# By-token products for gates, merge and MLP of a hybrid decoder block, with seven block products in place of eight in three of the eight k pairs of the MLP's first product

## The chip, the core and the metric

The kernel runs on one core of a Trainium2 chip, in fp32. TensorE (PE) multiplies: a 128x128 stationary operand is loaded (PEld), and up to 512 columns of a moving operand stream through it into a PSUM bank of 128x512 fp32, of which there are eight. VectorE (DVE) and ScalarE (ACT) work element by element, GpSimd (POOL) does a little of that and issues some DMAs, SyncE (SP) issues the loads of the weights. The metric is device time in microseconds (us) of one execution.

## The reference, cut to what matters

For 256 tokens of 2048 features:

```
h = rms_norm(x) ; proj = h @ w_in                      # 2048 x 18576
gate_att, gate_ssm, q, k, v, q_idx, k_idx, w_idx, z, xbc, dt = split(proj)
att = top-k sparse attention(q, k, v, q_idx, k_idx, w_idx)     # 16 heads
y   = gated, normed state-space mixer(z, conv(xbc), dt)        # 4096 wide
merged = sigmoid(gate_att) * (att @ w_att) + sigmoid(gate_ssm) * (y @ w_ssm)
x = x + merged @ w_out
x = x + square(relu(rms_norm(x) @ w_up)) @ w_down      # w_up 2048 x 8192
```

## The kernel before

Each fp32 operand is split into a rounded part `hi` (fp32r) and a rest `lo`; a product is hi\*hi + hi\*lo + lo\*hi. `split` (L106, L107) makes the two parts of a weight chunk of 128x1024: a copy on ACT and a difference on DVE. `load` (L115) fetches the chunk through SP's queue into one of four `raw` buffers; `hi` and `lo` have three buffers each.

There are two forms of matrix product. `gemm_t` gives the result by feature (128 features on the partitions): for each k tile of 128 and each 128 features it takes the weights as stationary operand, `hi` against 512 moving columns (the 256 tokens' hi and lo side by side, L122) and `lo` against 256 columns (L123). Such a couple of matmuls, 512 and 256 columns, I call a pair of instructions. Its evacuation, `halves` (L175, L176), adds the two halves of the bank. `gemm_a` gives the result by token (128 tokens on the partitions): the activations are stationary and the weights move, three matmuls of 512 columns for each k tile, 128 tokens and 512 features (L148). For 128 tokens x 512 features x 128 k that is 1536 columns; `gemm_t` streams 768 columns for 256 tokens x 128 features x 128 k, so both forms stream the same number of columns for the same work, in 3 instructions by token and 4 by feature.

By feature run: the index queries, the two gate projections (`C_GA`, `C_GS`), B, C and x of the mixer, `w_att`, `w_ssm`, `w_out` and `w_up`. By token run q, k, v, z and `w_down`. At the start x is loaded by token into `xt` and turned on PE by 32 transposes (L285); g1\*x is the moving operand of the first two groups, while `h_first` (L340 to L343) makes the normed `hl` that all later products use; a small product of 144 columns (L408, L410) follows. In the MLP `u` holds all 64 tiles of 128 hidden features by 256 tokens; `w_down` runs after that in two halves of its output columns over 64 k tiles, each bank started by four transposes of the residual (L950, 32 in all).

Work beside the products (scores, heads, the mixer, the convolution) is written as generators; `pump` runs a step of them after each chunk, by a credit of the stage. A scheduler then sets the order of each engine's instructions from its own timeline, except on DVE and ACT in the first group, which is written in order by hand. Two of the PSUM banks serve such side work (`aux_bank`), six the products (`main_bank`).

## Time and profile before

| | |
|---|---|
| median of 3 runs | 2000.99 us (2000.95 to 2001.97) |
| profiled execution, its own time | 2002.37 us |
| its span | 2000.6 us |
| PE busy | 1993.1 us (100%), 10693 instructions |
| DVE busy | 1376.6 us (69%) |
| ACT busy | 1055.0 us (53%) |
| POOL busy | 54.3 us (3%) |
| HBM traffic | 187 GB/s over the span |

The page gives busy time and share of each engine, a strip of 40 slices, the DMA queues, the chain of work that ended last, and the costliest groups of instructions. A PE instruction's own duration overlaps with the next one's, so the cost of a matmul in a row of matmuls is read from a stretch divided by its count, not from the mean of one. An fp32 matmul that is no transpose stands as two instructions in the profile.

### The profile page before, as it was taken

Reading aid. Unit: us, or ns where it says so; the run is one execution under the profiler, and the core shown is the slowest. Engines: PE = TensorE matmul, PEld = TensorE weight load, DVE = VectorE, ACT = ScalarE, POOL = GpSimd, SP = SyncE. Lnnn points to the kernel's source line nnn. Section 1 sums busy time; section 2 is a strip of 40 time slices with the busy share of each in tenths; the row PEclk is TensorE's granted clock in tenths of the full one; section 3 lists DMA queues with packets and bytes.
Section 4 is the critical chain, followed back from the end, with each engine's and each line's share of the span. In section 5 each row is a group of like instructions: output and inputs, shape, how many; then the busy total and the mean of one; then the engine's idle time right before and its main releaser. Section 6 shows DMA issues by size and latency. Waiting matters only on the chain.

```text
span 2000.6 us, 28778 instructions
## 1 busy us (share of the span) xinstructions
PE 1993.1 (100%) x10693; PEld 1702.4 (85%) x10693; DVE 1376.6 (69%) x2444; ACT 1055.0 (53%) x1730; POOL 54.3 (3%) x125
## 2 busy tenths in 40 slices
PE   9999999999999999999999999999999999999999
PEld 8878888888888888888888888888888888888887
DVE  8877766568888888888667677665555555555554
ACT  6555655444555554555656665555544445455444
POOL 2002000000000000000000000000000000000000
PEclk9999999999999999999999999999999999999999
DMA  7647555566555665555555555655555555556553
GB/s 261 201 144 220 174 160 162 170 220 190 182 183 175 187 192 175 188 183 169 190 183 189 188 188 199 201 193 189 187 191 189 189 189 190 189 191 210 194 199 133
DMA packets 172850, 375.35 MB, mean 188 GB/s; under 512 B 16787, under 2 KB 17637, under 8 KB 172709
## 3 DMA queue, kind: packets, MB, share of 16 engines
q1 hardware_dynamic: 168004, 357.97, 55.4%
q0 software_dynamic: 4704, 15.54, 2.8%
q8 instruction: 84, 1.38, 0.3%
q14 instruction: 58, 0.47, 0.1%
HBM read 368.42 MB, written 5.05 MB: 187 GB/s over the span
## 4 chain that ended last, share of the span: by engine, by line
PE 99%; DMA 0%; DVE 0%; SPq 0%; issue 0%; ACT 0%; DVEq 0%; ACTq 0%
PE mb L122 40%; PE mb L148 33%; PE mb L123 20%; PE ab L804 1%; PE ab L492 0%; PE ab L748 0%; PE ab L823 0%; PE ab L600 0%; PE ab L796 0%; PE ab L768 0%; PE ab L625 0%; DMA xt<-in_x_dram 0%; PE mb L408 0%; PE ab L621 0%; PE ab L757 0%; PE ab L599 0%
## 5 line engine op out<-in xcount | busy, mean ns | idle before, releaser
L107 DVE TENSOR_TENSOR lo<-raw,hi 128x1024 fp32r<-128x1024 f32 x664 | 811.3, 1224 | 555.8 <-ACT hi L106 552.1
L106 ACT CAST hi<-raw 128x1024 fp32r<-128x1024 f32 x664 | 697.8, 1052 | 748.1 <-PE mb L122 402.0
L122 PE MATMUL mb<-h_hl,hi 128*128 128x512 f32 x1280 | 439.9, 397 | 0.0
L122 PE MATMUL mb<-x_hl,hi 128*128 128x512 f32 x1024 | 343.4, 394 | 0.0
L123 PE MATMUL mb<-h_hl,lo 128*128 128x256 f32 x1280 | 342.0, 286 | 0.0
L148 PE MATMUL mb<-hi,uhl 128*128 128x512 f32 x1024 | 316.9, 390 | 0.0
L148 PE MATMUL mb<-hi,h_hl 128*128 128x512 f32 x896 | 280.5, 392 | 0.0
L122 PEld LDWEIGHTS mb<-h_hl,hi 128*128 128x128 f32 x1280 | 236.2, 188 | 50.5 <-issue 1.9
L123 PE MATMUL mb<-x_hl,lo 128*128 128x256 f32 x1024 | 261.6, 279 | 0.0
L123 PEld LDWEIGHTS mb<-h_hl,lo 128*128 128x128 f32 x1280 | 236.2, 189 | 8.3 <-issue 1.9
L148 PEld LDWEIGHTS mb<-hi,uhl 128*128 128x128 f32 x1024 | 192.2, 188 | 39.7
L122 PEld LDWEIGHTS mb<-x_hl,hi 128*128 128x128 f32 x1024 | 186.3, 188 | 37.8
L148 PE MATMUL mb<-lo,uhl 128*128 128x512 f32 x512 | 199.3, 389 | 0.0
L148 PEld LDWEIGHTS mb<-hi,h_hl 128*128 128x128 f32 x896 | 167.4, 188 | 36.6 <-issue 2.3
L123 PEld LDWEIGHTS mb<-x_hl,lo 128*128 128x128 f32 x1024 | 187.7, 188 | 7.2
L122 PE MATMUL mb<-yhl,hi 128*128 128x512 f32 x512 | 180.3, 398 | 0.6 <-DVE yhl L877 0.4
L148 PE MATMUL mb<-lo,h_hl 128*128 128x512 f32 x448 | 176.2, 393 | 0.0
L123 PE MATMUL mb<-yhl,lo 128*128 128x256 f32 x512 | 142.2, 280 | 0.0
L122 PEld LDWEIGHTS mb<-yhl,hi 128*128 128x128 f32 x512 | 95.8, 188 | 24.8 <-DVE yhl L877 2.1
L148 PEld LDWEIGHTS mb<-lo,uhl 128*128 128x128 f32 x512 | 96.1, 188 | 19.8
L148 PEld LDWEIGHTS mb<-lo,h_hl 128*128 128x128 f32 x448 | 84.1, 188 | 18.3 <-issue 1.3
L123 PEld LDWEIGHTS mb<-yhl,lo 128*128 128x128 f32 x512 | 96.5, 189 | 0.5
(264 smaller groups left out, 2032.0 us busy)
## 6 DMA issues: line engine op xcount, KB each, us to landing
raw<-in_w_in_dram SPq DMA_DIRECT2D x288, 512.0 KB, 3.5
raw<-in_w_down_dram SPq DMA_DIRECT2D x64, 1024.0 KB, 5.2
raw<-in_w_up_dram SPq DMA_DIRECT2D x60, 1024.0 KB, 5.2
raw<-in_w_ssm_branch_dram SPq DMA_DIRECT2D x64, 512.0 KB, 3.9
raw<-in_w_att_branch_dram SPq DMA_DIRECT2D x32, 512.0 KB, 3.8
raw<-in_w_out_dram SPq DMA_DIRECT2D x32, 512.0 KB, 4.0
abc<-acum_d POOLq DMA_DIRECT2D x16, 512.0 KB, 5.0
raw<-in_w_up_dram SPq DMA_DIRECT2D x8, 512.0 KB, 4.5
```

The costliest lines, as they stand in the source:

```text
L106: a.copy(hi, raw)
L107: v.tensor_tensor(lo, raw, hi.bitcast(F32), op=OP.subtract)
L122: pe.matmul(banks[j], hi[:, js], mv, start=kk == 0, stop=False)
L123: pe.matmul(banks[j][:, :S], lo[:, js], mv[:, :S], start=False, stop=kk == nk - 1)
L148: pe.matmul(banks[t][c], st[:, x_ + t * P:x_ + (t + 1) * P], w_[:, c * 512:(c + 1) * 512], start=kk == 0 and i == 0 and not started, stop= ...
L804: pe.matmul(yd[:, i * 64:(i + 1) * 64], M[:, i], xk[c][:, i * 64:(i + 1) * 64], start=True, stop=True)
```

## The change

- The gate projections (`C_GA`; `C_GS` in the same way, in `gates`), `w_att`, `w_ssm`, `w_out` and `w_up` are computed by token. `gemm_a` with chunks of 128x1024 takes the place of `gemm_t`; the evacuations become one operation of 512 columns per bank.
- What a later product needs by feature is turned on PE: `merged` (32 transposes, `merged_task`), the new x (32, `norm_task`), the squared hidden features (128, `u_task`).
- `w_up` is done by `mixed` in eight groups of 1024 features, over eight pairs of k tiles. For one pair, 2 token blocks x 2 feature blocks x 2 k tiles make eight block products. `UP = "NSNSNSNN"` sets the kind of a pair: N does the eight, S does seven products of sums of blocks. All of them accumulate in seven PSUM banks (`q`), so that N has to be written in S's terms: it adds into the banks 2, 5, 3 and 4 and uses the difference of the two token blocks as a third stationary operand. `combine` makes the four results of the seven banks. `left` makes the sums on the activations' side (POOL, then hi and lo), once for the kernel, `pieces_s` those on the weights' side, in every group.
- The MLP runs in two halves of its hidden features: `up(0)`, `down(0)`, `up(1)`, `down(1)`; `u` is half as large. `w_down` has the k tiles of a half, and the residual is added on DVE at its evacuation instead of by transposes on PE.
- In the MLP the PSUM banks are divided into seven for products and one for side work.
- x is handed over by feature (`x_t`), with vectors, convolution taps and the table of the attention's bias laid out; the transposes of x at the start, the small ones of the vectors and the bias product fall away. In the first group the sums of squares come from ACT and POOL on `x_t`, and the reciprocal root is made after the group.

```diff
+UP = "NSNSNSNN"
...
+                    a.activation(ssx, xT[:, :2], AF.Square)
+                else:
+                    sq = ap_.tile([P, 2, S], F32, name=nm("sq"), tag="bt", bufs=3)
+                    a.activation(sq, xT[:, k:k + 2], AF.Square)
+                    nc.gpsimd.tensor_tensor(ssx, ssx, sq, op=OP.add)
...
-        matt = low.tile([P, KT, S], F32, name="matt", tag="matt")
-        for g in range(4):
-            def ev(j, bank, g=g):
-                m = matt[:, 4 * g + j]
-                halves(ap_, bank, m)
-                a.activation(m, m, AF.Tanh, scale=0.5)
-            gemm_t(w_in, C_GA + g * 512, KT, h_mv, ev, RATE)
+        matt = low.tile([P, 2, D], F32, name="matt", tag="matt")
+        for g in range(2):
+            banks = [[main_bank(), main_bank()] for _ in range(2)]
+            for t, c in gemm_a(wide(w_in, C_GA + g * 1024), KT, h_mv, banks, RATE):
+                c0 = g * 1024 + c * 512
+                a.activation(matt[:, t, c0:c0 + 512], banks[t][c], AF.Tanh, scale=0.5)
...
-        for g in range(4):
-            def ev(j, bank, g=g):
-                t = ap_.tile([P, S], F32, name=nm("ao"), tag="ao", bufs=2)
-                halves(ap_, bank, t)
-                m = matt[:, 4 * g + j]
-                v.scalar_tensor_tensor(m, m, 1.0, t, op0=OP.add, op1=OP.mult)
-            gemm_t(w_att, g * 512, KT, lambda kk: att_hl[:, kk], ev, RATE)
+        for g in range(2):
+            banks = [[main_bank(), main_bank()] for _ in range(2)]
+            for t, c in gemm_a(wide(w_att, g * 1024), KT, lambda kk: att_hl[:, kk], banks, RATE):
+                c0 = g * 1024 + c * 512
+                m = matt[:, t, c0:c0 + 512]
+                v.scalar_tensor_tensor(m, m, 1.0, banks[t][c], op0=OP.add, op1=OP.mult)
...
+        def merged_task(g, ms):
+            for c in range(2):
+                transposed(lambda t: ms[t][c], 8 * g + 4 * c, to_mhl)
+                yield 2500
+
+        for g in range(2):
+            if g:
+                tg = gates(g)
+            banks = [[main_bank(), main_bank()] for _ in range(2)]
+            ms = [[None, None], [None, None]]
+            for t, c in gemm_a(wide(w_ssm, g * 1024), 32, y_mv, banks, 500):
+                c0 = g * 1024 + c * 512
+                m = ms[t][c] = mp.tile([P, 512], F32, name=nm("m"), tag="m", bufs=4)
+                v.scalar_tensor_tensor(m, tg[:, t, c * 512:(c + 1) * 512], 1.0, banks[t][c],
+                                       op0=OP.add, op1=OP.mult)
+                v.tensor_tensor(m, m, matt[:, t, c0:c0 + 512], op=OP.add)
+            queue.append(merged_task(g, ms))
...
+        LEFT_S = {1: 0, 2: 1, 3: 3, 5: 4, 7: 6, 6: 5, 4: 2}
+        LEFT_N = {2: (0, 0), 5: (1, 1), 3: (2, 1), 4: (1, 0)}
+
+        def left(kind, pool, src, hi, lo):
+
+            d = pool.tile([P, 4, P], F32, name=nm("d"), tag="d", bufs=2)
+            g = nc.gpsimd
+            if kind == "S":
+                a11, a12, a21, a22 = src[:, 0, 0], src[:, 1, 0], src[:, 0, 1], src[:, 1, 1]
+                g.tensor_tensor(d[:, 1], a21, a22, op=OP.subtract)
+                g.tensor_tensor(d[:, 2], d[:, 1], a11, op=OP.subtract)
+                g.tensor_tensor(d[:, 0], d[:, 2], a12, op=OP.add)
+                g.tensor_tensor(d[:, 3], a11, a21, op=OP.subtract)
+                parts = ((slice(0, 2), src[:, :, 0]), (2, a22), (slice(3, 7), d))
+            else:
+                g.tensor_tensor(d[:, :2], src[:, :, 0], src[:, :, 1], op=OP.subtract)
+                hi, lo = (z.rearrange("p (k n) t -> p k n t", n=3) for z in (hi, lo))
+                parts = (((slice(None), slice(0, 2)), src), ((slice(None), 2), d[:, :2]))
+            for at, x_ in parts:
+                at = (slice(None), *at) if isinstance(at, tuple) else (slice(None), at)
+                a.copy(hi[at], x_)
+                v.tensor_tensor(lo[at], x_, hi[at].bitcast(F32), op=OP.subtract)
...
+        def norm_task(g):
+            for j in range(4 * g, 4 * g + 4):
+                b = aux_bank()
+                for i in range(2):
+                    for t in range(2):
+                        c0 = (2 * j + i) * P
+                        pe.transpose(b[:, i * S + t * P:i * S + (t + 1) * P],
+                                     xn[:, t, c0:c0 + P], ident)
+                x_ = scratch[0].tile([P, 2, 2, P], F32, name=nm("xf"), tag="ev",
+                                     bufs=1 if scratch[0] is mp else 5)
+                for i in range(2):
+                    m = 2 * j + i
+                    a.mul(x_[:, i], b[:, i * S:(i + 1) * S].rearrange("p (t n) -> p t n", t=2),
+                          vec[:, G2 + m:G2 + m + 1])
+                z = XA[g][:, xa_at[j]:xa_at[j] + (7 if UP[j] == "S" else 6)]
+                left(UP[j], scratch[0], x_, z[:, :, :P], z[:, :, P:])
+                xa_done.add(j)
+                yield 2500
...
+        psum_stack.close()
+        psum[:] = [enter(tc.tile_pool(name="psum2", bufs=1, space=PSUM)), 7]
...
+            r0, r1 = (load(w, kk + i, 1, c0, 1024)[:, 0] for i in range(2))
+            h1 = fp.tile([P, 512], F32R, name=nm("h1"), tag="h1", bufs=1)
+            l1 = fp.tile([P, 512], F32R, name=nm("l1"), tag="l1", bufs=1)
+            a.copy(h1, r0[:, :512])
+            v.tensor_tensor(l1, r0[:, :512], h1.bitcast(F32), op=OP.subtract)
+            h2, l2 = (z[:, 0] for z in split(r1, [P, 1, 1024]))
+            t13 = fp.tile([P, 2, 512], F32, name=nm("t13"), tag="t13", bufs=1)
+            v.tensor_tensor(t13[:, 0], r0[:, :512], r0[:, 512:], op=OP.add)
+            v.tensor_tensor(t13[:, 1], r0[:, 512:], r1[:, 512:], op=OP.add)
+            h3, l3 = split(t13, [P, 2, 512])
+            t24 = fp.tile([P, 2, 512], F32, name=nm("t24"), tag="t24", bufs=1)
+            v.tensor_tensor(t24[:, 0], t13[:, 0], r1[:, 512:], op=OP.add)
+            v.tensor_tensor(t24[:, 1], t24[:, 0], r1[:, :512], op=OP.add)
+            h4 = fp.tile([P, 2, 512], F32R, name=nm("h4"), tag="h4", bufs=1)
+            l4 = fp.tile([P, 2, 512], F32R, name=nm("l4"), tag="l4", bufs=1)
+            a.copy(h4, t24)
+            v.tensor_tensor(l4, t24, h4.bitcast(F32), op=OP.subtract)
+            return {1: (h1, l1), 2: (h2[:, :512], l2[:, :512]), 3: (h2[:, 512:], l2[:, 512:]),
+                    5: (h3[:, 0], l3[:, 0]), 7: (h3[:, 1], l3[:, 1]),
...
+        def mixed(kinds, w, k0, c0, operands, rate):
+
+            q = {i: main_bank() for i in (1, 6, 7, 2, 5, 3, 4)}
+            left_of = {i: sum(1 if kind == "S" else 2 * (i in LEFT_N) for kind in kinds)
+                       for i in q}
+            total = dict(left_of)
+
+            def product(i, hi, lo, whi, wlo):
+                for n, (st, mv) in enumerate(((hi, whi), (hi, wlo), (lo, whi))):
+                    pe.matmul(q[i], st, mv, start=left_of[i] == total[i] and n == 0,
+                              stop=left_of[i] == 1 and n == 2)
+                left_of[i] -= 1
+
+            for j, kind in enumerate(kinds):
+                hi, lo = operands(j)
+                kk = k0 + 2 * j
+                if kind == "S":
+                    ws = pieces_s(w, kk, c0)
+                    for i, s_ in LEFT_S.items():
+                        product(i, hi[:, s_], lo[:, s_], *ws[i])
+                else:
+                    ws = pieces_n(w, kk, c0)
+                    last = j == len(kinds) - 1
+                    todo = [(i, k) for k in range(2) for i in LEFT_N]
+                    if last:
+                        todo.sort(key=lambda x_: list(LEFT_N).index(x_[0]))
+                    for i, k in todo:
+                        s_, c = LEFT_N[i]
+                        s_ += 3 * k
+                        cs = slice(c * 512, c * 512 + 512)
+                        product(i, hi[:, s_], lo[:, s_], ws[k][0][:, cs], ws[k][1][:, cs])
+                pump(rate)
+            return q
...
+            q1 = block()
+            a.copy(q1, q[1])
+            u2 = plus(q[6], q1)
+            u3 = plus(q[7], u2)
+            v.tensor_tensor(out_[0][0], q[2], with_(q1, 0, 0), op=OP.add)
+            t5 = plus(q[5], u2, OP.subtract)
+            if before is None:
...
+            v.tensor_tensor(out_[0][1], q[3], with_(t5, 0, 1), op=OP.add)
+            v.tensor_tensor(out_[1][0], q[4], with_(u3, 1, 0), op=OP.add)
...
+        def u_task(g, cs):
+
+            for c in range(2):
+                for t in range(2):
+                    a.activation(cs[t][c], cs[t][c], AF.Relu, scale=rstd2[:, t:t + 1])
+                for j2 in range(2):
+                    b = aux_bank()
+                    for j in range(2):
+                        for t in range(2):
+                            f0 = (2 * j2 + j) * P
+                            pe.transpose(b[:, j * S + t * P:j * S + (t + 1) * P],
+                                         cs[t][c][:, f0:f0 + P], ident)
+                    m = 8 * g + 4 * c + 2 * j2
+                    a.activation(u[:, m:m + 2], b.rearrange("p (m s) -> p m s", m=2), AF.Square)
+                    yield 5000
+
+        def up(h):
+            for g in range(4):
+                q = mixed(UP, w_up, 0, h * MH + g * 1024, x_operands, 5000)
+                cs = [[fp.tile([P, 512], F32, name=nm("c"), tag="c", bufs=4) for _ in range(2)]
+                      for _ in range(2)]
+                combine(q, cs)
+                queue.append(u_task(g, cs))
...
+        def down(h):
...
+                for t, c in gemm_a(d_pieces, MH // P, u_st, banks, 2500,
+                                   tail=2 if h and c2 else 0):
+                    c0 = c2 * 1024 + c * 512
+                    x_ = xn[:, t, c0:c0 + 512]
+                    if h == 0:
+                        v.tensor_tensor(x_, banks[t][c], x_, op=OP.add)
+                        continue
+                    o = fp.tile([P, 512], F32, name=nm("o"), tag="c", bufs=4)
+                    v.tensor_tensor(o, banks[t][c], x_, op=OP.add)
+                    nc.sync.dma_start(out2[t * P:(t + 1) * P, c0:c0 + 512], o)
+
+        for h in range(2):
+            up(h)
+            down(h)
```

Of its 10,425 matmul instructions as built the program keeps 9,201. 2560 of the 3456 pairs of `gemm_t` are gone; `gemm_a` has 5184 matmuls instead of 2880, and `mixed` (L973) has 1464.

On DVE, in `w_up` before, between two groups of 512 features: `lo` of the weight chunks, and the evacuations of the banks (`up`).

```order
L176 TENSOR_TENSOR up_2666_14215<-mb_2640_14033,half_2667_14216 128x256
L933 SCALAR_TENSOR_TENSOR up_2664_14209<-up_2664_14209,rb2_12135 128x256
L933 SCALAR_TENSOR_TENSOR up_2666_14215<-up_2666_14215,rb2_12135 128x256
L107 TENSOR_TENSOR lo_2681_14276<-raw4_2679_14273,hi_2680_14275 128x1024
L176 TENSOR_TENSOR up_2668_14221<-mb_2641_14034,half_2669_14222 128x256
L933 SCALAR_TENSOR_TENSOR up_2668_14221<-up_2668_14221,rb2_12135 128x256
L107 TENSOR_TENSOR lo_2683_14296<-raw4_2679_14273,hi_2682_14295 128x1024
L107 TENSOR_TENSOR lo_2686_14318<-raw4_2684_14315,hi_2685_14317 128x1024
```

On DVE, in `w_up` now, in a group's third and fourth pair of k tiles (N, then S): `raw_2351` and `raw_2354` are the N pair's chunks, `raw_2358` and `raw_2359` the S pair's; `t13` and `t24` are sums of weight blocks, `l1` and `l4` the rests of the blocks that have no `lo` buffer.

```order
L950 TENSOR_TENSOR t13_2364_12211<-raw_2358_12199 128x512
L951 TENSOR_TENSOR t13_2364_12211<-raw_2358_12199,raw_2359_12201 128x512
L111 TENSOR_TENSOR lo_2353_12160<-raw_2351_12157,hi_2352_12159 128x1024
L954 TENSOR_TENSOR t24_2367_12218<-t13_2364_12211,raw_2359_12201 128x512
L947 TENSOR_TENSOR l1_2361_12204<-raw_2358_12199,h1_2360_12203 128x512
L111 TENSOR_TENSOR lo_2356_12166<-raw_2354_12163,hi_2355_12165 128x1024
L1077 TENSOR_TENSOR uhl_2585_13171<-u_11623,uhl_2585_13171 128x256
L955 TENSOR_TENSOR t24_2367_12218<-t24_2367_12218,raw_2359_12201 128x512
L1077 TENSOR_TENSOR uhl_2591_13206<-u_11623,uhl_2591_13206 128x256
L111 TENSOR_TENSOR lo_2363_12208<-raw_2359_12201,hi_2362_12207 128x1024
L111 TENSOR_TENSOR lo_2366_12215<-t13_2364_12211,hi_2365_12214 128x1024
L959 TENSOR_TENSOR l4_2369_12222<-t24_2367_12218,h4_2368_12221 128x1024
```

The two `lo` of the N pair have the sums for the S pair between them, and ahead of PE's use `uhl` tiles of the coming `w_down`. Where two chunks gave two rows before, an S pair now gives eight.

On PE, in `w_up` before, at a group's k tile: four banks (`mb_2670` to `mb_2673`) in turn.

```order
L122 MATMUL mb_2670_14227<-x_hl_12133,hi_2682_14295 128x512
L122 MATMUL mb_2671_14228<-x_hl_12133,hi_2682_14295 128x512
L122 MATMUL mb_2672_14229<-x_hl_12133,hi_2682_14295 128x512
L122 MATMUL mb_2673_14230<-x_hl_12133,hi_2682_14295 128x512
L123 MATMUL mb_2670_14227<-x_hl_12133,lo_2683_14296 128x256
L123 MATMUL mb_2671_14228<-x_hl_12133,lo_2683_14296 128x256
L123 MATMUL mb_2672_14229<-x_hl_12133,lo_2683_14296 128x256
L123 MATMUL mb_2673_14230<-x_hl_12133,lo_2683_14296 128x256
```

On PE, in `w_up` now, at the first pair of k tiles (N) of the second group: `mb_2326` to `mb_2329` are the banks 2, 5, 3 and 4 of the group.

```order
L973 MATMUL mb_2326_12048<-hi_2334_12060,xa0_10901 128x512
L973 MATMUL mb_2327_12049<-hi_2334_12060,xa0_10901 128x512
L973 MATMUL mb_2328_12050<-hi_2334_12060,xa0_10901 128x512
L973 MATMUL mb_2326_12048<-lo_2335_12061,xa0_10901 128x512
L973 MATMUL mb_2326_12048<-hi_2334_12060,xa0_10901 128x512
L973 MATMUL mb_2327_12049<-lo_2335_12061,xa0_10901 128x512
L973 MATMUL mb_2327_12049<-hi_2334_12060,xa0_10901 128x512
L973 MATMUL mb_2328_12050<-lo_2335_12061,xa0_10901 128x512
L973 MATMUL mb_2328_12050<-hi_2334_12060,xa0_10901 128x512
L973 MATMUL mb_2329_12051<-hi_2331_12054,xa0_10901 128x512
L973 MATMUL mb_2329_12051<-lo_2332_12055,xa0_10901 128x512
L973 MATMUL mb_2329_12051<-hi_2331_12054,xa0_10901 128x512
```

Three of the group's banks are taken in turn, and the fourth, `mb_2329`, comes 18 matmuls later than the first: it is the bank that waits for a result of the group before to be read.

## Rows read from the trace of the kernel before

**Rows 1.** The page: busy time of engines; granted clock; the chain that ended last.

```profile
PE 1993.1 (100%) x10693; PEld 1702.4 (85%) x10693; DVE 1376.6 (69%) x2444; ACT 1055.0 (53%) x1730; POOL 54.3 (3%) x125
...
PEclk9999999999999999999999999999999999999999
...
PE 99%; DMA 0%; DVE 0%; SPq 0%; issue 0%; ACT 0%; DVEq 0%; ACTq 0%
```

**Rows 2.** Busy time (count) in stretches: mixer, w_up, w_down; clock, DMA share, GB/s.

```profile
408.00:955.00 547.00, 547.00 (x3004) 468.76 (x3003) 448.79 (x927) 278.37 (x408) 18.67 (x64) 1.00 0.59 185
1273.00:1630.00 357.00, 357.00 (x2049) 311.71 (x2048) 208.37 (x281) 178.36 (x264) 0.00 (x0) 1.00 0.59 190
1630.00:2000.60 370.60, 366.23 (x1651) 303.82 (x1649) 207.24 (x267) 180.28 (x267) 0.00 (x0) 1.00 0.55 187
```

**Rows 3.** The chain that ended last: start us, us, engine, tile, line, count.

```profile
921.91 0.87 PE ab L823 x8
...
1825.72 170.52 PE mb L148 x752
```

**Rows 4.** PE's groups by line and shape: count, busy us, mean ns.

```profile
L122 PE MATMUL mb<-h_hl,hi 128*128 128x512 f32 x1280 | 439.9, 397 | 0.0
L122 PE MATMUL mb<-x_hl,hi 128*128 128x512 f32 x1024 | 343.4, 394 | 0.0
...
L122 PE MATMUL mb<-yhl,hi 128*128 128x512 f32 x512 | 180.3, 398 | 0.6 <-DVE yhl L877 0.4
...
L122 PE MATMUL mb<-att_hl,hi 128*128 128x512 f32 x256 | 87.7, 398 | 0.1
L122 PE MATMUL mb<-mhl,hi 128*128 128x512 f32 x256 | 85.3, 396 | 0.0
...
L950 PE MATMUL mb<-ident,xn 128*128 128x128 f32 x32 | 5.1, 272 | 0.0
...
L285 PE MATMUL ab<-ident,xt 128*128 128x128 f32 x16 | 3.5, 355 | 0.9 <-DMA xt<-in_x_dram 0.9
...
L285 PE MATMUL mb<-ident,xt 128*128 128x128 f32 x16 | 2.5, 281 | 0.3 <-DMA xt<-in_x_dram 0.3
```

**Rows 5.** DVE's groups by line and shape: count, busy us, mean ns, idle before.

```profile
L107 DVE TENSOR_TENSOR lo<-raw,hi 128x1024 fp32r<-128x1024 f32 x664 | 811.3, 1224 | 555.8 <-ACT hi L106 552.1 <-PE ab L588 1.3 <-PE mb L122 1.1
...
L806 DVE TENSOR_TENSOR y<-ab,y 128x512 f32<-128x512 f32 x16 | 11.0, 687 | 0.1
...
L340 DVE SCALAR_TENSOR_TENSOR h<-xT,vec,rb 128x256 f32<-128x256 f32 x16 | 7.6, 479 | 0.0
...
L343 DVE TENSOR_TENSOR h_hl<-h,h_hl 128x256 fp32r<-128x256 f32 x16 | 6.4, 419 | 0.0
...
L189 DVE SCALAR_TENSOR_TENSOR rs_t<-rs_t,rs_m 128x2 f32<-128x2 f32 x27 | 4.2, 157 | 0.3
...
L403 DVE TENSOR_TENSOR hi<-raw,hi 128x288 fp32r<-128x288 f32 x8 | 3.6, 450 | 0.4 <-ACT hi L402 0.2
```

**Rows 6.** ACT's groups by line and shape: count, busy us, mean ns, idle before.

```profile
L106 ACT CAST hi<-raw 128x1024 fp32r<-128x1024 f32 x664 | 697.8, 1052 | 748.1 <-PE mb L122 402.0 <-PE mb L148 284.7 <-issue 39.9
```

**Rows 7.** DMA issues: count, KB each, median us from issue to landing.

```profile
raw<-in_w_in_dram SPq DMA_DIRECT2D x288, 512.0 KB, 3.5
...
raw<-in_w_out_dram SPq DMA_DIRECT2D x32, 512.0 KB, 4.0
...
xt<-in_x_dram SPq DMA_DIRECT2D x4, 128.0 KB, 3.3
```

**Rows 8.** The start in order of time: start us, us, what.

```profile
8.06 2.07 PE L122 MATMUL mb<-xg,hi 128*128 128x512 f32 x4
```

**Rows 9.** Line 408: duration ns min/median/max, first and last start us.

```profile
L408 PE MATMUL mb<-hi,h_hl x32: 293/340/377, 58.0 to 65.6; 128*128 128x288 f32 x32
```

**Rows 10.** DVE's groups from 10 to 25 us, where POOL is busy.

```profile
L306 DVE TENSOR_TENSOR lo<-raw,hi 128x1024 fp32r<-128x1024 f32 x5 | 9.5, 1899 | 0.0
```

**Rows 11.** The same stretch, busy time (count) of PE, PEld, DVE, ACT, POOL.

```profile
10.00:25.00 15.00, 14.68 (x93) 12.82 (x93) 13.72 (x20) 13.14 (x31) 10.39 (x8) 1.00 0.99 352
```

373 lines of the change are left out of this document (166 added, 207 removed).

## The prediction, made before the changed kernel ran

> **What bounds the kernel now.** I read the page first [rows 1]. PE is busy 1993.1 of 2000.6 us, the chain that ended last is 99% PE, and the granted clock is full, which is the 2.4 GHz level, from end to end. DVE (69%) and ACT (53%) have room. So a PE instruction taken away is time taken away, as long as DVE keeps up. Then I read the stretches [rows 2]: even in the mixer, where DVE is busy 448.8 of 547.0 us (82%), PE is busy for the whole 547.0. In `w_up` DVE is busy 58% and POOL does nothing. Third, I read what a PE instruction costs in a row of its like: the `w_up` stretch holds 2049 PE instructions in 357.00 us, that is 1024 pairs of 512 and 256 columns, 348.6 ns a pair [rows 2]; `w_down`, by token, has 752 matmuls of 512 columns in 170.52 us, 226.8 ns each [rows 3].
>
> **Part 1: by feature to by token.** A pair streams 768 columns, which is 1.5 matmuls by token, 340.1 ns. The gain is 8.5 ns a pair. The pairs that go are the counts of 512-column matmuls [rows 4]: 512 of the 1280 from `h_hl` (both gates), 256 `att_hl`, 512 `yhl`, 256 `mhl`, 1024 `x_hl`, in sum 2560. That is 2560 x 8.5 ns = **-21.8 us**.
>
> The Trainium skill ("TensorE: Matmul & The Clock Gate", section "Back-to-back issue gap") gives for an isolated warm matmul the columns divided by 2.4, plus 2.5 ns: an estimate from it is 325 ns for a pair and 323.8 for 1.5 matmuls, a gain of 1.3 ns and 3.3 us in all, and the kernel would come out at 1999.7. The stretches above are 5% longer than that in both forms and differ more among themselves. The measurement decides.
>
> **Part 2: seven products for eight.** Eight groups with three S pairs each leave out one block product of three matmuls: 72 matmuls x 226.8 ns = **-16.3 us**. An N pair has its 24 matmuls as `gemm_a` would; the detour through S's banks adds none.
>
> **Part 3: transposes.** A row of eight 128-column transposes took 0.87 us, 108 ns each [rows 3]. Added are 32 (`merged`), 32 (x) and 128 (`u`); removed are 32 of L950 and 32 of L285 (16 into `ab`, 16 into `mb`) [rows 4]. Net 128 x 108 ns = **+13.8 us**. The small transposes of vectors and taps and the bias product go too: I take **-1** (0 to -2).
>
> **Part 4: the head.** The first product started at 8.06 us [rows 8], behind x's transposes. Now x comes by feature, and a 128 KB piece of x lands 3.3 us after its issue [rows 7], so some 5.5 us is possible. That is 2.5 us, and the transposes that stood among the first products (32 x 0.108 = 3.5 us in all) go. Against it stands DVE. The reciprocal root is now made behind the first group, and only then `h_first` can run: 16 x (479 + 419) ns = 14.4 us. With it are due eight `lo` (9.8 us), eight operations on banks at about 0.42 (3.3), the small product's eight splits (3.6), and the root and its spreading (about 2.8): 34 us of DVE [rows 5], while PE has one group of about 22 us and no other work. The small product's last matmul started at 65.6 us [rows 9]; I expect 61.5: **-4** (0 to -6).
>
> **Part 5: DVE in the new `w_up`.** This is where the gain can be lost. For a group of 1024 features DVE has 10 `lo` for five N pairs and 9 for three S pairs, 19 x 1.224 us, and 22 operations of 512 columns (l1 and four sums in each S pair, seven in `combine`). The trace has no sum of two SBUF operands of that width; I price them by `y` of 128x512, 687 ns, and not by half of a `lo`, 612 [rows 5]. In sum 23.3 + 15.1 = 38.4 us. PE has 183 matmuls and 16 transposes, 41.5 + 1.7 = 43.2 us. So DVE is 89% busy, above the mixer's 82%. ACT has about as many elements to cast at 1052 ns and stays near 27 us of 43 [rows 6]; it is no rival. Inside the group it isn't even: an S pair needs 7.1 us of DVE for 4.76 of PE, an N pair 2.45 for 5.44. N stands before S so that DVE can work ahead, as far as the four `raw` and three `lo` buffers let it; `h1`, `l1`, `t13`, `t24`, `h4` and `l4` have one buffer each. I walked the built order through a group with these durations: PE waits some 0.25 us for the first S pair's `h3`, and some 0.6 us for the first `lo` of the fifth pair, together 0.9 a group. At the group's start PE enters three banks and comes to the fourth 18 matmuls (4.1 us) later, and `combine` has read that one after about 2.3 us; no stall there. The first group also has the `left` work on DVE for the S pairs (about 7 us with the root of the second norm): 45.4 of DVE against 43.2 of PE, 2.2 us late. Stalls: 2.2 + 7 x 0.9 = **+8.5** (0 to 54.5, the top being rival A's).
>
> POOL has a part here. In the stretch from 10 to 25 us POOL is busy 10.39 of 15 us [rows 11], and a `lo` took 1899 ns instead of 1224 [rows 10]: five of them lose 3.4 us, a third of POOL's busy time. POOL now makes `left`'s differences (some 3.4 us of POOL in the first group) and, in the head, the sums of squares. By the row DVE loses about 1.1 us in the first group, which is in the 2.2 above.
>
> The Trainium skill ("SBUF — State Buffer", section "Who interferes with whom") says that a DVE operation with two SBUF inputs and a GpSimd operation that reads SBUF exclude each other on a shared port pair. The row shows a third of that; by the rule the whole 3.4 us would be lost once, and the forecast would be 2.3 us higher.
>
> **Part 6: the rest.** The PSUM pools change hands ahead of the MLP, and `down(0)` and `down(1)` each begin on banks that `combine` has to free: **+1** (0 to 2). Weights are read as often as before. A 512 KB chunk lands 3.5 to 4.0 us after issue [rows 7] and `w_up` moved 190 GB/s at a DMA share of 0.59 [rows 2]; in a kernel 1% shorter that grows by 1%. `w_down`'s residual moves from PE to an operation that replaces an evacuation of equal size, and costs nothing.
>
> **Sum.** -21.8 - 16.3 + 13.8 - 1 - 4 + 8.5 + 1 = -19.8 us. The profiled execution has a span of 2000.6 and an own time of 2002.37, 1.4 above the median of the runs. I take its differences from the median: 2000.99 - 19.8 = **1981**.
>
> **Rivals.**
> *A, DVE sets the pace in `w_up`.* With one buffer for `t13`, `t24`, `h4` and `l4`, at each of the 24 S pairs PE waits for a cast (1.05) [rows 6] and a difference (1.22) [rows 5] made only after the buffer is free: 24 x 2.27 = 54.5 in place of 8.5, **2027**. It turns the change slower as soon as a pair costs more than (19.8 + 8.5) / 24 = 1.2 us. For it: 89% busy, S pairs that need 7.1 us of DVE in 4.76 of PE. Against it: N pairs between them give back 3 us each, the mixer at 82% didn't wait, and in the order the next S pair's sums stand among the N pair's `lo`.
> *B, the conversion gives nothing.* If the 8.5 ns belong to what ran beside the two stretches (`w_up` against `w_down`) and not to the form, part 1 is 0: **2003**. For it: the two rates come from different stretches. Against it: the `w_down` stretch has as much DVE work (207 us) and 187 GB/s [rows 2], and is the faster. The Trainium skill's formula of part 1 would end close to B; by that formula neither stretch would have its length.
> *C, no stall, and the head gains 6.* 1981 - 8.5 - 2 - 1 and a little from the vectors: **1968** or less.
> *That the change doesn't do what it says* is not open: as built it has 9,201 matmul instructions for 10,425 and L973's 1464 is 1536 less 72.
>
> **How the numbers follow.** Forecast (stalls of 0 to 2.5 us a group): 1968 to 1996, chance 0.66. A: 0.22, of which 0.07 within 0.2% (4 us, about what a measurement here can tell from no change) and 0.15 above. B: 0.07, same. C below 1968: 0.05. Faster 0.71, same 0.14, slower 0.15. The range runs from 1968 to 2004, leaving out C and the upper part of A, 0.2.
>
> **What would show it.** The cadence of L152 and L973 in an unbroken row should be 227 ns, and the stretches of the gates, `w_att`, `w_ssm` and `w_out` shorter by 2.4% plus their transposes at 108 ns; a cadence of 232 is B. A group of `w_up` should take about 44 us with DVE busy at 85 to 90%; PE's waits should name `lo` (L111), `h3` and `l4` (L959). If a group takes 50 us, A is right. The small product should end at about 62 us. The prediction is wrong if a sum of 512 columns costs far more than 687 ns, or if PE is slower between banks that change with every third matmul than in `w_down`.

## The result, and the profile of the changed kernel

The changed kernel takes 1988.39 us (median of 4 runs, 1988.21 to 1988.68) against 2001.48 us of the kernel before beside it (2000.95 to 2002.49): ratio 0.9936, 95% interval 0.9923 to 0.9948. That is 13.1 us faster, where 19.8 were forecast; the time lies in the range. The profiled execution has a span of 1987.0 us, 13.6 less than the 2000.6 of before.

The page of the changed kernel has these lines where before has [rows 1]: the engines' busy time, and the shares of the chain that ended last.

```profile
PE 1973.6 (99%) x9473; PEld 1641.5 (83%) x9473; DVE 1418.3 (71%) x2335; ACT 1041.4 (52%) x1566; POOL 56.8 (3%) x110
...
PE 96%; DVE 2%; ACT 1%; DMA 1%; issue 0%; POOL 0%; SPq 0%; DVEq 0%; ACTq 0%; POOLq 0%
```

PE is still the bound, but it is now idle for 13.4 us, where before it was for 7.5, and the chain has stretches of DVE, ACT and DMA. What PE waited for longest (engine, line, what it waited for, total us, times, longest):

```profile
PE mb L973 <- DVE xn L919: 2.2, 1, 2.2
PE mb L127 <- DVE lo L287: 2.0, 2, 1.0
PE mb L126 <- ACT hi L277: 1.8, 1, 1.8
```

The first wait is at the entry of the MLP, the other two are in the first group. To see where time went I cut both spans at the same places: the first use of a product's stationary or moving operand. These are the first and last starts on PE (us, behind the durations in ns), first of before, then of after.

```profile
L122 PE MATMUL mb<-att_hl,hi x256: 387/395/579, 324.4 to 420.8; 128*128 128x512 f32 x128
L122 PE MATMUL mb<-yhl,hi x512: 387/395/505, 968.6 to 1198.1; 128*128 128x512 f32 x171
L122 PE MATMUL mb<-mhl,hi x256: 387/395/403, 1195.6 to 1286.5; 128*128 128x512 f32 x128
L122 PE MATMUL mb<-x_hl,hi x1024: 387/395/477, 1286.8 to 1644.6; 128*128 128x512 f32 x171
```

```profile
L152 PE MATMUL mb<-hi,att_hl x256: 387/389/499, 322.2 to 420.5; 128*128 128x512 f32 x128
L152 PE MATMUL mb<-hi,yhl x512: 389/389/389, 968.4 to 1187.6; 128*128 128x512 f32 x171
L152 PE MATMUL mb<-hi,mhl x256: 387/389/476, 1187.8 to 1278.4; 128*128 128x512 f32 x128
L973 PE MATMUL mb<-hi,xa x832: 387/389/628, 1281.0 to 1805.8; 128*128 128x512 f32 x167
L152 PE MATMUL mb<-hi,uhl x1024: 387/389/479, 1457.9 to 1981.8; 128*128 128x512 f32 x171
```

The small product ends at 66.0 before and 66.8 after. From these ends the stages, and what the terms of the forecast give for each:

| stage | before, us | after, us | measured | forecast |
|---|---|---|---|---|
| head, to the small product's end | 66.0 | 66.8 | +0.8 | -7.5 |
| q, k, v, gates, `w_att` (to 421.2 / 420.7) | 355.2 | 353.9 | -1.3 | -5.4 |
| mixer and first half of `C_GS` (to 968.6 / 968.4) | 547.4 | 547.7 | +0.3 | -1.1 |
| rest of `C_GS`, `w_ssm`, `w_out` (to 1286.8 / 1278.8) | 318.2 | 310.4 | -7.8 | -2.4 |
| MLP, with its entry | 713.8 | 708.2 | -5.6 | -3.4 |

The forecast's column is its own terms put where they belong (8.5 ns for each pair, 108 ns for each transpose, 3.5 us for L285 and 4 for the head, 8.5 and 1 us for stalls and pools). So the head fell 8.3 us short and the next two stages 5.5; the last two did 7.6 better.

### The profile page after: what moved, and what is told of

Read it like the earlier page. It is cut to its first block, busy times and chain, and to the rows that moved or that the text cites. A ratio compares the mean times of both kernels' runs of the same rounds, so it can differ in the third digit from the quotient of the medians.

```text
span 1987.0 us, 26274 instructions
## 1 busy us (share of the span) xinstructions
PE 1973.6 (99%) x9473; PEld 1641.5 (83%) x9473; DVE 1418.3 (71%) x2335; ACT 1041.4 (52%) x1566; POOL 56.8 (3%) x110
## 4 chain that ended last, share of the span: by engine, by line
PE 96%; DVE 2%; ACT 1%; DMA 1%; issue 0%; POOL 0%; SPq 0%; DVEq 0%; ACTq 0%; POOLq 0%
PE mb L152 59%; PE mb L973 15%; PE mb L126 10%; PE mb L127 5%; PE ab L747 1%; PE ab L1058 1%; PE ab L457 1%; DVE lo L111 1%; DMA raw<-in_w_in_dram 0%; PE ab L766 0%; PE ab L691 0%; PE ab L739 0%; PE ab L711 0%; PE ab L551 0%; PE ab L576 0%
## 5 line engine op out<-in xcount | busy, mean ns | idle before, releaser
L152 PE MATMUL mb<-hi,h_hl 128*128 128x512 f32 x1408 | 444.1, 393 | 0.0
L152 PE MATMUL mb<-lo,h_hl 128*128 128x512 f32 x704 | 278.1, 395 | 0.3 <-DVE lo L111 0.3
L973 PE MATMUL mb<-hi,xa 128*128 128x512 f32 x832 | 263.0, 392 | 2.6 <-DVE xn L919 2.2
L126 PE MATMUL mb<-h_hl,hi 128*128 128x512 f32 x768 | 262.5, 396 | 0.0
L127 PE MATMUL mb<-h_hl,lo 128*128 128x256 f32 x768 | 204.2, 286 | 0.0
L973 PEld LDWEIGHTS mb<-hi,xa 128*128 128x128 f32 x832 | 156.9, 189 | 35.8 <-ACT sq L922 2.6
L973 PE MATMUL mb<-lo,xa 128*128 128x512 f32 x416 | 164.4, 395 | 0.2
L152 PE MATMUL mb<-hi,yhl 128*128 128x512 f32 x512 | 158.0, 389 | 0.0
L152 PEld LDWEIGHTS mb<-hi,yhl 128*128 128x128 f32 x512 | 96.1, 188 | 20.0
L152 PE MATMUL mb<-lo,yhl 128*128 128x512 f32 x256 | 99.6, 389 | 0.0
L973 PEld LDWEIGHTS mb<-lo,xa 128*128 128x128 f32 x416 | 78.4, 189 | 17.2 <-DVE lo L111 1.3
```

What stands on the lines that cost most here:

```text
L126: pe.matmul(banks[j], hi[:, js], mv, start=kk == 0, stop=False)
L127: pe.matmul(banks[j][:, :S], lo[:, js], mv[:, :S], start=False, stop=kk == nk - 1)
L152: pe.matmul(banks[t][c], st[:, x_ + t * P:x_ + (t + 1) * P], w_[:, c * 512:(c + 1) * 512], start=kk == 0 and i == 0 and not started, stop= ...
L973: pe.matmul(q[i], st, mv, start=left_of[i] == total[i] and n == 0, stop=left_of[i] == 1 and n == 2)
```

## The experiments

Each kernel below is the changed kernel with one edit, unless it says more. The changed kernel's 1988.39 us is compared with their medians; the kernel before had 2001.89, 2001.32, 2002.44 and 2001.19 us in the four sets of runs, so differences under about 1 us are not told apart.

### The first group as it was before

The edit puts back the loads of x by token, `prepare` with its 32 transposes, and the sums of squares of before:

```diff
+        xt = ap_.tile([P, 2, D], F32, name="xt", tag="qT")
         xT = low.tile([P, KT, S], F32, name="xT", tag="matt")
...
+            prepare(0)
             for p in range(KT // 2):
+                if p + 1 < KT // 2:
+                    prepare(p + 1)
```

> The changed kernel with the first group of before: x loaded by token and turned on PE (32 transposes), the sums of squares and the reciprocal root made within the group. Theory 1 (the forecast, which put 4 us for the head and 3.5 us for its transposes): 7.5 us slower, 1996. Theory 2 (the start is bound by the loads, by ACT and by DVE, which is what the trace of after shows until 26 us and again from 57 to 66 us; transposes on PE lie in its idle time): within 1.5 us of after, 1987 to 1990.

Measured: 1982.62 us, 5.8 us *faster* than the changed kernel, so neither theory held. The traces tell where. The small product ends at about the same time in both (last start 66.0 in this run, 66.5 in after): the two heads are equal, which is theory 2. But `att_hl` is first used at 316.6 in place of 322.2. Between 90 and 155 us stand the scores of the index heads. This is the chain in that stretch, by line, of before, of after and of this run, where the scores are L492, L457 and L473:

```profile
by line: PE mb L148 81.7%; PE ab L492 14.3%; PE ab L588 2.2%; PE ab L536 1.1%; PE ab L470 0.4%; PE ab L472 0.3%; PE ab L471 0.2%
```

```profile
by line: PE mb L152 79.2%; PE ab L457 18.1%; PE ab L539 2.0%; PE ab L435 0.4%; PE ab L436 0.4%; PE ab L437 0.3%
```

```profile
by line: PE mb L152 84.6%; PE ab L473 11.8%; PE ab L555 2.9%; PE ab L451 0.4%; PE ab L453 0.3%; PE ab L452 0.2%
```

The same 64 instructions hold 9.3, 11.8 and 7.7 us of the chain. Their pieces in order of time say why (start us, length us, line, count), two of after and one of this run:

```profile
104.70 0.85 PE ab L457 x4
105.55 1.12 PE mb L152 x4
106.68 0.85 PE ab L457 x4
```

```profile
102.63 0.86 PE ab L473 x8
```

A score has a contraction over 64 rows; one head of a couple lies on rows 0 to 63, the other on rows 64 to 127. Eight instructions of both heads together take as long as four of one. In before there are five groups of eight, in after two, in this run seven. None of these lines is in the diff. The scheduler places a head's scores when its side bank comes free, and I take it that an edit in the head shifts those moments; no run shows that step by itself.

### The scores of two heads kept together

```diff
-                for ts, ks, ds in ((slice(0, P), slice(0, P), slice(0, P)),
-                                   (slice(P, S), slice(0, S), slice(P, 384))):
-                    for i in range(2):
...
+                with tc.manual_schedule(engines={mybir.EngineType.PE}):
+                    for ts, ks, ds in ((slice(0, P), slice(0, P), slice(0, P)),
+                                       (slice(P, S), slice(0, S), slice(P, 384))):
+                        for i in range(2):
```

> The changed kernel with one thing more: the four score matmuls of two heads (contraction over 64, head one on rows 0 to 63, head two on rows 64 to 127) are kept together on PE. In the trace a group of eight instructions of both heads takes 0.86 us and a group of four of one head 0.85; before has 5 groups of eight and 6 of four, after 2 and 12, head_old 7, 1 and 2 halves. Theory 1 (the order in which the scores fell, and not the head's own work, is most of what head_old gained): 65 us hold 11.8 us of scores in after and would hold 7.5: 3.5 to 4.5 us faster than after, 1984 to 1985. Theory 2 (side by side or not, the scores lie in a stretch that something else sets, DVE's accumulation of them): within 1 us of after.

Measured: 1982.84 us (1982.75 to 1982.94), 5.5 us faster than the changed kernel. The chain from 90 to 155 us of this run, by line, and two of its score pieces:

```profile
by line: PE mb L152 86.2%; PE ab L458 11.6%; PE ab L540 1.3%; PE ab L435 0.4%; PE ab L436 0.4%; PE ab L437 0.3%
...
124.56 0.86 PE ab L458 x8
130.18 0.86 PE ab L458 x8
```

The scores hold 7.5 us (11.6% of 65), 4.3 less than in after, and `att_hl` is first used at 316.7, 5.5 us earlier. Six of the eight couples of heads now stand as eight in a row; two are still parted into two and six. Theory 1 holds, with 1 us more than it forecast. 1.2 us of the 5.5 are not in the scores' own pieces; what else moved there I did not single out. With the scores in order the new head (1982.84) and the old one (1982.62) are equal within what the runs can tell: the head's rework was worth nothing.

### Gates and `w_att` by feature again

The gate projection `C_GA` and `w_att` go through `gemm_t` with the evacuations of before:

```diff
-            for t, c in gemm_a(wide(w_att, g * 1024), KT, lambda kk: att_hl[:, kk], banks, RATE):
...
+            gemm_t(w_att, g * 512, KT, lambda kk: att_hl[:, kk], ev, RATE)
```

> The changed kernel with the gate projection of the attention (C_GA) and w_att by feature again, everything else as in after; their results are merged unturned, so that part of the output isn't the reference's, and no work is left out. Theory 1 (the forecast: 8.5 ns for each of 512 pairs): 4.4 us slower than after, 1992.8. Theory 2 (the heads of the attention set this stretch: by token they ran 21 us later into w_att, and the matmuls of 360 to 374 us stand 264 ns apart in place of 227, so the gain of the form was given back there): 0 to 1.5 us slower, 1988.4 to 1990.

Measured: 1991.08 us, 2.7 us slower, between the theories: 5.3 ns a pair. The scores have the order of after here, two groups of eight and twelve of four, so for the two products together this is a clean comparison. Where each of them begins and ends does not divide it:

```profile
L126 PE MATMUL mb<-att_hl,hi x256: 387/395/579, 327.3 to 423.6; 128*128 128x512 f32 x128
```

Up to the start of `w_att` the run is 5.1 us later than after (327.3 against 322.2); `w_att` takes 96.3 us from first to last start, and 98.3 in after. But work of the heads moved from one product to the other: of their matmul instructions (L550, L551, L572, L576, L578) 44 stand within `w_att` in this run and 66 in after. In after's chain two of them take 0.22 us (L550, L578) or 0.43 (L551, L576), and three of L572 0.33, so the 22 more are about 3.3 us, which is an estimate. Without them `C_GA` gains some 1.8 us by token and `w_att` 1.3, where the forecast has 2.2 for each. In after the heads' results come late in `w_att` (engine's tile, chain in order of time):

```profile
360.24 1.04 ACT hi L110
361.29 0.28 ACT att_hl L580
361.57 0.04 issue
361.61 2.11 PE mb L152 x8
```

PE goes on with the product only behind ACT's `att_hl`, and the next eight matmuls take 264 ns each; the same comes once more, at 366.42. That the heads set this stretch is what theory 2 says, and the trace bears it out for these places in `w_att` alone; the larger part of theory 1's gain came.

### `C_GS` and `w_ssm` by feature again

```diff
-            for t, c in gemm_a(wide(w_ssm, g * 1024), 32, y_mv, banks, 500):
...
+            gemm_t(w_ssm, g * 512, 32, y_mv, ev, 0)
+            if g < 2:
+                gemm_t(w_in, C_GS + (g + 2) * 512, KT, h_mv, ev_gate(g + 2), 0)
```

> The changed kernel with C_GS and w_ssm by feature again; the gated attention is added unturned, so that the output isn't the reference's; no transposes of merged then (32 less). Theory 1 (the forecast's 8.5 ns a pair): 768 x 8.5 ns - 32 x 108 ns = +3.0 us, 1991.4. Theory 2 (in this stretch a pair costs more than in w_up: 227.0 us for 640 pairs in the trace of before, 354.7 ns, against 228.5 ns x 1.5 by token): 768 x 12 to 14 ns - 3.5 = +6 to +7 us, 1995.

Measured: 1994.74 us, 6.3 us slower. With the 3.5 us of transposes that this run doesn't have, the pairs are worth 9.8 us, 12.8 ns each: theory 2. The stretch of `w_ssm` in this run and, by token, the chain of after (first line: us, PE, PEld, DVE, ACT, POOL busy, clock, DMA share, GB/s):

```profile
968.00:1194.00 226.00, 225.36 (x1285) 195.99 (x1285) 159.34 (x264) 142.36 (x253) 0.00 (x0) 1.00 0.63 189
```

```profile
1073.01 115.16 PE mb L152 x508
```

By feature that is 226.00 us for 642 pairs, 352 ns each, against 348.6 in `w_up` [rows 2]; by token 226.7 ns a matmul, 340.0 for one and a half. DVE is 71% busy here by feature and 57% by token, but PE is idle for only 0.6 us, 1 ns a pair, so waits do not explain the 352, and why a pair costs more here than in `w_up` stays open.

### `w_up` by feature again

S, N, the sums and the transposes of the squared features go; x is made by feature as `x_hl`, `w_up` runs through `gemm_t`, and the two halves of the features stay.

```diff
-                q = mixed(UP, w_up, 0, h * MH + g * 1024, x_operands, 5000)
...
+                gemm_t(w_up, h * MH + g * 512, KT, moving, ev, 5000)
```

> The changed kernel with w_up by feature again (no S and N pairs, no sums of blocks, no transposes of the squared features), still in halves of the features. Theory 1 (the forecast's prices): +8.7 us for 1024 pairs, +16.3 for the block products, -13.8 for the transposes, and 4 to 6 us of DVE's lateness and of the lower clock at the start of w_up gone: +5 to +7 us, 1994 to 1995.5. Theory 2 (the whole gain of the change is in w_up; what was won elsewhere was lost again): +10 us or more, 1998 or slower.

Measured: 1995.48 us, 7.1 us slower, at the upper end of theory 1: the forecast's prices for form, block products and transposes together. None of the three is measured alone by this run.

### One S pair, four S pairs, three in a row

```diff
-UP = "NSNSNSNN"
+UP = "NSNNNNNN"
```

> The changed kernel with one S pair of the eight instead of three (UP = NSNNNNNN). Sixteen pairs go back to eight block products, 48 matmuls more. Theory 1 (an S pair is worth its three matmuls, 0.68 us, and DVE is late in the first group alone, as the trace of after reads): 16 x 0.68 = +10.9 us less up to 2 us in the first group, so 9 to 11 us slower than after, 1997 to 1999, and the groups of w_up other than the first at about 44.5 us. Theory 2 (the forecast's 0.9 us of waiting in each of the groups, which would go with the S pairs): +10.9 - 5 = +6 us, 1994.

Measured: 1997.49 us, 9.1 slower for 16 pairs fewer, 0.57 us for each S pair; its three matmuls are 0.68. Theory 1. For all 24 pairs that makes an estimate of 13.6 us, of the 16.3.

```diff
-UP = "NSNSNSNN"
+UP = "NSNSNSNS"
```

> The changed kernel with a fourth S pair in place of the last N pair (NSNSNSNS). PE has 24 matmuls less, 5.4 us. Theory 1 (DVE is now the bound of a group: 38.4 + 4.7 = 43.1 us by the forecast's durations against 42.5 us of PE, and the last S pair has the sums of combine right behind it): no gain or a loss, 1988 to 1998, DVE busy 95% or more in w_up. Theory 2 (PE stays the bound): -5 us, 1983.

Measured: 1985.93 us, 2.5 faster where the matmuls alone would give 5.4; between the theories. In this run PE waits for DVE and ACT, for all but 0.2 us of it in the first group and about the start of the second, between 1303 and 1329 us:

```profile
PE mb L973 <- DVE lo L111: 2.0, 4, 1.0
...
PE mb L973 <- ACT h L946: 0.9, 1, 0.9
```

```diff
-UP = "NSNSNSNN"
+UP = "NNSSSNNN"
```

> The changed kernel with the same three S pairs side by side (NNSSSNNN for NSNSNSNN): the same count of matmuls, the same DVE work in a group. Theory 1 (DVE can work ahead only as far as the single buffers of t13, t24, h4 and l4 let it): three S pairs need 21.3 us of DVE beside 14.3 us of PE, one pair can be made ahead, so PE waits 2 to 4 us in each of 8 groups: +16 to +32 us, 2004 to 2020, with PE's waits at L111 and L959. Theory 2 (only the share over a group counts): within 2 us of after, 1986 to 1990.

Measured: 1992.86 us, 4.5 slower: neither theory. The first half of `w_up` shows where. It lasts from 1281.2 to 1463.1 us, 5.0 longer than in after, and its first group has these windows (us, PE, PEld, DVE, ACT, POOL busy, clock, DMA share, GB/s):

```profile
1303.00:1307.00 4.00, 1.49 (x8) 0.91 (x6) 2.81 (x5) 1.00 (x2) 2.97 (x1) 0.98 0.13 17
1307.00:1311.00 4.00, 3.59 (x9) 2.82 (x10) 3.61 (x4) 3.51 (x7) 1.82 (x1) 0.50 0.33 120
```

PE stands still for 2.9 us where the left side's sums for x lie beside the three S pairs, and goes on at the lower level of the clock. What it waits for begins on POOL (one row each of POOL, ACT and PE; in brackets the idle time before it and what ended it):

```profile
1300.25 5.72 POOL L872 TENSOR_TENSOR d<-xf 128x256 f32<-128x256 f32 x1 [4.50 <-ACT xf L902]
```

```profile
1306.00 0.40 ACT L877 CAST xa<-d 128x256 fp32r<-128x256 f32 x1 [4.28 <-POOL d L872]
```

```profile
1307.41 1.22 PE L973 MATMUL mb<-hi,xa 128*128 128x512 f32 x2 [2.92 <-ACT hi L110]
```

One `d` of `left` takes 5.72 us, where the other four of its shape take 1.00 to 1.82; DVE's operations follow each other without a pause from before its start until 1305.4, and each of them reads two operands in SBUF. ACT stands behind that `d`, and the `hi` that PE needs comes only after it. So in this trace it is POOL beside DVE that sets the wait, rather than the single buffers. The profiled execution, 1995.66 us, is the slowest of the five: the three with a mean clock of 1.000 took 1991.51 to 1992.86, so the lower clock is no part of the median's 4.5 us. The other groups lose little in the trace: DVE works further ahead than the single buffers made me think, and the interleaving of N and S is worth something mainly in the first group.

### The entry of the MLP

In after the first matmul of `w_up` waits for the last evacuation of `w_out`, whichever bank that is in: the wait belongs to the closing of the PSUM pool. The granted clock then falls to 0.50, the 1.2 GHz level, for between 3 and 4 us. Columns as above, of after, and the piece of the chain that begins there:

```profile
1280.00:1282.00 2.00, 1.04 (x4) 0.88 (x5) 2.00 (x4) 2.00 (x7) 0.00 (x0) 0.96 0.58 213
1282.00:1284.00 2.00, 2.00 (x6) 1.58 (x5) 1.65 (x5) 0.95 (x3) 0.00 (x0) 0.50 0.07 18
1284.00:1286.00 2.00, 2.00 (x7) 1.60 (x7) 1.93 (x7) 0.44 (x1) 0.00 (x0) 0.69 0.37 55
```

```profile
1280.96 7.29 PE mb L973 x24
```

The first 24 matmuls take 7.29 us, where 24 at 226.8 ns are 5.44. The first try to avoid it gave the two side banks a tag each in one pool that lasts to the end:

```diff
-        psum_stack.close()
-        psum[:] = [enter(tc.tile_pool(name="psum2", bufs=1, space=PSUM)), 7]
...
-            q = {i: main_bank() for i in (1, 6, 7, 2, 5, 3, 4)}
+            q = {i: main_bank() for i in (2, 5, 3, 4, 6, 7)}
+            q[1] = aux_bank(0)
```

> The changed kernel with one PSUM pool to the end: the two side banks have a tag each, and in the MLP one of them serves as the seventh bank of a group, so that no pool is closed between w_out and w_up and the first product waits for its own banks alone. Theory 1: PE's idle 2.2 us there and the 4 us at the lower granted clock behind it (about 1.9 us lost) both come from the hand-over: 3 to 4 us faster than after, 1984.5 to 1985.5, and the granted clock stays 1.00. Theory 2: ACT and DVE are as late with the first hi and lo of w_up and the drop of the clock stays: at most 1 us faster.

Measured: 1991.18 us, 2.8 slower. The edit touched the side banks of the whole kernel, and the order of everything ahead of the MLP with them: the scores fell into fifteen groups of four and none of eight, and the MLP began later than in after. So it was made again with a pool of its own for the side banks, which leaves that order as it is:

```diff
-        psum[:] = [enter(tc.tile_pool(name="psum2", bufs=1, space=PSUM)), 7]
+        aux[:] = [aux_stack.enter_context(tc.tile_pool(name="aux2", bufs=1, space=PSUM)), 1]
...
+            q[1] = aux[0].tile([P, 512], F32, name=nm("mb"), tag="seventh", bufs=1)
```

> The changed kernel with the side banks in a PSUM pool of their own, so that only that pool changes hands ahead of w_up; all work ahead of the MLP stands in the order of after (which the run entry did not keep). Theory 1 (the hand-over of the pool is the cause of the idle 2.2 us and of the lower clock behind it): 3 to 4 us faster than after, 1984.5 to 1985.5. Theory 2 (what was saved at the entry is lost in the first group, where DVE has the sums of the left side as well as the pairs' work; entry's first half of w_up was 2.1 us longer than after's): 0 to 2 us faster.

Measured: 1989.08 us (1987.25 to 1990.26), no gain. The idle time and the low clock at the entry are gone, and come back as something else. This run's windows and its second longest wait:

```profile
1270.00:1290.00 20.00, 20.00 (x94) 16.47 (x93) 15.52 (x23) 14.14 (x25) 1.25 (x2) 1.00 0.59 164
1290.00:1310.00 20.00, 17.32 (x77) 12.96 (x76) 17.84 (x30) 12.26 (x20) 8.17 (x6) 1.00 0.51 158
```

```profile
PE ab L898 <- ACT xf L904: 1.8, 1, 1.8
```

PE is busy throughout until 1290 and then idle for 2.7 us: theory 2, though the rows name POOL ahead of DVE. A `d` of 128x128 takes 3.06 us where the shortest of its line takes 0.64, the next one 2.53, and ACT, whose next `xf` has to read the side bank before PE can fill it again, stands still for 5.42 us ahead of it:

```profile
1290.60 3.06 POOL L868 TENSOR_TENSOR d<-xf 128x128 f32<-128x128 f32 x1
```

```profile
1296.84 0.62 ACT L879 CAST xa<-d 128x512 fp32r<-128x512 f32 x1 [5.42 <-POOL d L870]
```

What PE did earlier, it waited for later, since the left side's sums of the second half of x set when the fifth to eighth pair can begin. The traced execution is the fastest of the five; the four others took 1989.06 to 1990.26. The executions of after point the same way for the clock: one had a mean clock of 1.000 and 1988.21 us, the three others 0.998 or 0.999 and 1988.30 to 1988.68. So the time at the lower level there seems to be for the most part time in which the left side comes up; no run separates the two.

### Together

Four edits at once, the old head, the scores together, the fourth S pair and the pool of the side banks:

> Four edits together: the first group of before (head_old), the score matmuls of two heads kept together, a fourth S pair (NSNSNSNS) and the side banks in a pool of their own. If the gains add up: 5.8 (head_old, which holds most of what the scores give) + 0.5 (the rest of the scores) + 2.5 (fourth pair) + 1 to 3.5 (entry) = 10 to 12 us faster than after, 1976.5 to 1978.5. If the fourth pair and the entry draw on the same DVE time in the first group: 1979 to 1981.

Measured: 1988.82 us, none of the sum. The part ahead of the MLP kept its gain (`att_hl` first used at 316.5), and the MLP lost it. In the MLP PE has these waits, of which the longest lies in the second half:

```profile
PE mb L993 <- ACT h L965: 3.7, 4, 2.5
...
PE mb L993 <- DVE lo L113: 2.1, 4, 1.1
```

From 1634 to 1810 us PE was busy 172.68 of 176 us. The first half of `w_up` lost time as well: 181.5 us from the first use of x to the first use of the squared features, against 176.3 in `s_four`, with POOL's `d` again at 3.04 us and a wait of 1.8 us for `xf`. That the fourth pair and the other banks do this together is argued and not shown, since no run has these two alone. The last run leaves the banks and the head as in after:

```diff
-UP = "NSNSNSNN"
+UP = "NSNSNSNS"
...
+                with tc.manual_schedule(engines={mybir.EngineType.PE}):
```

> The changed kernel with the score matmuls of two heads kept together and a fourth S pair (NSNSNSNS), and nothing else. Theory (the two gains lie 1,100 us apart and draw on nothing in common): 5.5 + 2.5 = 8 us faster than after, 1980.4. Rival (the fourth pair costs as much as in the run of four edits, where the second half of w_up had PE idle for 3.3 us): 1983 to 1985, no better than the scores alone.

Measured: 1981.40 us (1979.90 to 1982.35), ratio 0.9900 to the kernel before (0.9884 to 0.9917): 7.0 us faster than the changed kernel and the fastest of all, but only 1.4 us better than the scores alone, which is little more than the runs can tell. It lies nearer to the theory (1980.4) than to the rival, so the loss in the run of four edits needs the banks or the old head as well as the fourth pair.

## Why the prediction was right, and where it was not

The direction, the range and the bound were right: PE stays the bound, the change takes instructions from it, and DVE does not take the bound over (rival A). Of the 19.8 us, 13.1 came. Part by part:

- **Part 1, the form.** Near in sum, wrong in its parts. By token a matmul costs 226.7 ns in `w_ssm` as in `w_down` [rows 3]. By feature a pair costs 348.6 ns in `w_up` [rows 2] but 352 in `w_ssm`, and by the two runs `C_GS` and `w_ssm` gained 12.8 ns a pair for 8.5, `C_GA` and `w_att` 5.3. The step that failed is taking one stretch's rate for all 2560 pairs. That these 1280 pairs come to 12.5 us where 10.9 were forecast is two errors of opposite sign, and so partly luck; for `w_out` and `w_up` the form was not run by itself. (The 348.6 ns are 7% above the 325 that the forecast estimates for a pair, not 5% as it says of both forms.) Rival B is refuted by the three runs by feature: each is slower, by 2.7, 6.3 and 7.1 us.
- **Part 2, seven for eight.** 0.57 us for each S pair, an estimated 13.6 us for 24, where 16.3 less the stalls of part 5 were forecast. Right, and better than forecast once the stalls are counted in.
- **Part 3, transposes.** Right at 108 ns: the four of `xn` at 1288.24 us take 0.44 us.
- **Part 4, the head.** Wrong. The forecast counted the 3.5 us of L285 twice, once in part 3 and once among the reasons for the 4 us of part 4. And neither came: the small product ended 0.8 us later than before. The first product started at 5.3 us in place of 8.1, but the chain then went over the third chunk's landing and ACT:

```profile
5.04 7.17 DMA raw<-in_w_in_dram
12.23 1.05 ACT hi L277
...
16.88 0.93 ACT hi L277
17.81 0.53 ACT sq L302
...
23.44 2.25 DVE lo L287
```

  The squares, half of which POOL made before and which are all on ACT now, stand between its casts, and a `lo` takes 2.25 us while POOL adds the squares. From 57 to 66 us the chain lies on DVE, which is the 34 us of DVE that part 4 counted and then priced at a gain.
- **Part 5, DVE in `w_up`.** Mis-sized, in the safe direction. DVE is 83% busy in the second half (142.34 of 172.00 us, columns as in the windows above), not 89:

```profile
1634.00:1806.00 172.00, 171.98 (x782) 141.77 (x781) 142.34 (x165) 100.99 (x119) 0.00 (x0) 1.00 0.59 197
```

  Its 732 matmuls at 226.8 ns and 48 transposes at 108 are 171.2 us and it took 172.1: 0.2 us a group, not 0.9. In the first half, from the first use of x, some 4 us were lost, about half of it to the clock. The Trainium skill ("SBUF — State Buffer", section "Who interferes with whom") says that whoever holds the shared port pair shuts the other out. Here POOL was the one that waited, as POOL's and DVE's rows of the first group show:

```profile
1298.28 3.06 POOL L867 TENSOR_TENSOR d<-d,xf 128x128 f32<-128x128 f32 x1
```

```profile
1298.14 1.21 DVE L959 TENSOR_TENSOR l<-t,h 128x1024 fp32r<-128x1024 f32 x1
1299.27 0.61 DVE L878 TENSOR_TENSOR xa<-xf,xa 128x256 fp32r<-128x256 f32 x2
1299.81 1.21 DVE L111 TENSOR_TENSOR lo<-t,hi 128x1024 fp32r<-128x1024 f32 x1
```

  A `d` whose shortest instance takes 461 ns took 3.06 us; DVE's operations with two operands in SBUF followed each other until 1301.0, and `d` ended at 1301.3. The trace agrees with that rule, and the forecast had looked only at DVE's side of it. In after PE lost nothing by this, since it waits for nothing between 1288 and 1335 us; in `s_row` and `entry2` it is where PE's longest wait in the first group began. Left's sums on DVE were not tried.
- **Part 6, the rest.** The change of PSUM pools was put at 1 us (0 to 2) and cost 2.2 of idle time and 1.85 at the lower clock on the spot. Avoiding it returned nothing, as `entry2` shows, since the first group's left side is late behind it anyway.
- **Not in the forecast at all:** the order of work that the change does not touch. The scores were split, 2.5 us worse in the chain than before, and put together they give 5.5 us. Of the 4.1 us by which the second stage of the table fell short, those 2.5 are the larger part; the 1.7 us that `C_GA` and `w_att` gave less than forecast are the rest. The 1.4 us that the third stage fell short stay open.

## What to carry to other kernels

With a scheduler that places instructions by its own timeline, a change moves work that it doesn't name: compare the built order of such work too, above all of small matmuls that are cheap only side by side. Take the rate of an instruction from the stretch that is changed, not from another with the same form, and book a saving in one part only. A wait removed at a stage's entry is worth nothing if the next thing the stage needs is late as well; follow that thing back past the engine that hands it over, here past ACT to POOL.
